# A guard inside the sum of squares, and a bank for each block of the last product

## The chip, the cores and the metric

The kernel runs on one core of a Trainium2 chip. The metric is the device time of one execution in microseconds (us). The engines are named as in the profile: PE (TensorE matmuls), PEld (its weight loads), DVE (VectorE), ACT (ScalarE), POOL (GpSimd), SP (SyncE, which issues most transfers).

## The reference

One step of a one-layer decoder over 2112 tokens (64 sample tokens and 2048 prompt tokens) of width 1024: a mixer of two kinds of linear recurrences, then a squared-ReLU MLP, then a final norm. What the change touches is the end of the layer and that norm:

```python
def rmsnorm(x, w):
    xf = x.astype(jnp.float32)
    r = xf * lax.rsqrt(jnp.mean(xf * xf, axis=-1, keepdims=True) + NORM_EPS)
    return (r * w.astype(jnp.float32)).astype(x.dtype)
...
        xp = xp + mp
        hp = rmsnorm(xp, norm_ffn_w[l])
        xp = xp + jnp.square(jax.nn.relu(hp @ w_up[l])) @ w_down[l]
...
    y_prompt = rmsnorm(xp, final_norm_w)
```

The guard of the last norm is `NORM_EPS` (1e-6).

## The kernel before, in words

**Layout.** Tokens are columns, features are partitions (8 blocks of 128). The tokens come in three groups of T = 512, 832 and 768. Each group runs through mixer, output projection (`out_proj`), MLP (`ffn`) and final norm. Weights and activations are held as two float32r parts (hi, lo), and each product is three matmuls (hi·hi, hi·lo, lo·hi). Work tiles are slabs of [128, 832] float32 out of a pool of 42. PSUM has a pool `pj` of two tiles of two banks each and a pool `mm` of four tiles of one bank.

**The scaled residual.** The norm ahead of the MLP is not applied to its input. Let q be mean(x²) + eps of the residual x. The squared ReLU of the unnormed input, multiplied by w_down, is q times too large, so the residual is multiplied by q instead (`scale_residual_first`, `scale_residual`), and everything after it carries the factor q. In the last norm this factor drops out of x/√mean(x²) but not out of the guard. The kernel before keeps g.r = 1/q (four reciprocals of a quarter each for every group, `inverse`), and `last_factor` multiplies the sum of squares by g.r² (L1662), takes Ln and Exp with the guard eps (L368, L369) and multiplies the result by g.r (L1664).

**The down product.** For groups 1 and 2 (`down`) the MLP's products are done by Strassen-like octets: for each of four octets seven products, each of two tiles v = 0, 1 with two blocks i = 0, 1 of 128 rows and T/2 = 384 columns (group 2). A tile [128, 2, 512] of `pj` holds the two blocks in two banks. DVE adds a finished tile to the accumulated rows (`put`, L1558). The last octet's order ends with S3·T3, A22·T4 and A12·B21; the last one completes the first half (h = 0) of feature blocks 0 to 3, A22·T4 that of blocks 4 to 7, S3·T3 the second half (h = 1). In the very last product of the kernel (`end`) each block is added for itself (L1588) so that its square (L1682) can start.

**Order.** The program is written with an agenda: `later(ticks, fn)` runs fn after so many ticks, and two matmuls make one tick, so one product of `down` is 24 ticks. The framework then orders the instructions of each engine by their place in the program and their readiness, and sets all waits.

**The final norm.** For groups 0 and 1 `finish_first` and `finish` run beside the next group's mixer. For group 2 `finish(g, (1,), 1)` treats h = 1 beside the last two products, with its adds of squares on POOL (L1625), the split of the sum into two parts (L1407, L1408), four matmuls with ones (L1416), the factor, and per block a multiplication by weight and factor (L1642) with a transfer for each pair of blocks (L1644). `finish_last` treats h = 0: squares and weights of each block on ACT (L1682, L1683), adds on POOL (L1685), the split (L498, L499), sums by matmul (float32r for six blocks, L1695, float32 for the last two, L1696), the factor, eight multiplications on DVE and POOL (L1705) and eight transfers (L1706).

Of the kernel before, what the change touches and what calls it, by code (L numbers as in the profile page):

```python
# [207 lines left out]
class Kernel:  # L208
# [972 lines left out]
    def scale_residual_first(self, g):  # L1181
# [19 lines left out]

        def inverse(i):
            if not i:
                g.r = self.get()
            c = slice(i * T // 4, (i + 1) * T // 4)
            nc.vector.reciprocal(g.r[:, c], x["q"][:, c])

# [4 lines left out]
        self.later(112, mean)  # L1212
        for i in range(4):
            self.later(194 + 20 * i, inverse, i)

# [36 lines left out]
    def finish_first(self, g):  # L1252

        nc, T = self.nc, g.T
        x = {"sum": None}

# [107 lines left out]
    def scale_residual(self, g):  # L1364
# [24 lines left out]

        def inverse(i):  # L1390
            if not i:
                g.r = self.get()
            c = slice(i * T // 4, (i + 1) * T // 4)
            nc.vector.reciprocal(g.r[:, c], x["q"][:, c])

# [6 lines left out]
        for i in range(4):  # L1402
            self.later(520 + 10 * i, inverse, i)

# [143 lines left out]
    def down(self, g, plan, nxt):  # L1548
# [14 lines left out]
        for o in range(NO):  # L1563
            last = o == NO - 1
            for A, B, first, into in LAST_OCTET if last else OCTET:
                self.plan_steps(plan, k, 0, 24)
                end = nxt is None and k == 7 * NO - 1
                if last and k % 7 == 3 and nxt is not None:
                    self.norm_in(nxt)
                if nxt is None and k == 7 * NO - 2:  # L1570
                    self.finish(g, (1,), 1)
                if end:
                    self.finish_last(g, 0)
                if first:
                    banks = [self.pj.tile([P, 2, 512], F32, tag="pj", name="pd")[:, :, :T2] for _ in range(2)]
                for v in range(2):
                    w = self.next_weight()
                    for i in range(2):
                        for e in range(2):
                            for f in range(2):  # L1580
                                c = (2 * e + f) * 256 + i * P
                                for q, (a, b) in enumerate(((0, 0), (0, 1), (1, 0))):
                                    self.matmul(banks[v][:, i], w[a][:, c:c + P], self.pair(g, g.d[o][e][B][b])[:, f],
                                                start=first and e == f == q == 0, stop=e == f == 1 and q == 2,
                                                skip_group_check=not first)
                        if end:
                            r = self.last_block(g, 2 * v + i, 0)
                            nc.vector.tensor_tensor(out=r, in0=banks[v][:, i], in1=r, op=ALU.add)  # L1588
                    if not end:
                        for q in into:  # L1590
                            put(v, "copy" if k == 0 else q, banks[v])
# [22 lines left out]

    def finish(self, g, hs=(0, 1), per=None):

# [4 lines left out]
        def square(np_, h):  # L1621
            t = self.get()
            nc.scalar.activation(t[:, :T], g.R[np_ % 2][np_ // 2, h][:, :T], AF.Square)
            if h in x:
                (nc.gpsimd if per else nc.vector).tensor_tensor(out=x[h][:, :T], in0=x[h][:, :T], in1=t[:, :T], op=ALU.add)  # L1625
            else:
                x[h] = t

        def split(h):
            x["parts", h] = self.pair_parts(g, x[h])  # L1630
            x["t", h] = self.get()
            nc.scalar.activation(x["t", h][:, :T2], g.r[:, h * T2:(h + 1) * T2], AF.Square)

        def factor(h):
            t = x["t", h][:, :T2]
            self.last_factor(g, self.pair_sums(g, x["parts", h]), t, t, h * T2, (h + 1) * T2, 0 if per else 4)

# [7 lines left out]

        pace, wait, gap, each = (3, 8, 6, 3) if per else (4, 8, 10, 5)
        t1 = 1 + pace * len(todo)
        for k, (np_, h) in enumerate(todo):
            self.later(1 + pace * k, square, np_, h)
            self.later(t1 + wait + gap + each * k, out, np_, h)  # L1650
        for h in hs:
            self.later(t1 + 2 * h, split, h)
            self.later(t1 + wait + 2 * h, factor, h)

# [4 lines left out]

    def last_factor(self, g, ps, r2, t, c0, c1, lag=0):  # L1660

        self.nc.vector.tensor_tensor(out=r2, in0=ps, in1=r2, op=ALU.mult)  # L1662
        self.rsqrt(t, r2, r2, self.eps, D)
        times = lambda: self.nc.vector.tensor_tensor(out=t, in0=t, in1=g.r[:, c0:c1], op=ALU.mult)  # L1664
        self.later(lag, times) if lag else times()

# [3 lines left out]

    def finish_last(self, g, h):

        nc, w = self.nc, g.T // 2
        order = (4, 5, 6, 7, 0, 1, 2, 3)
        when = [1, 2, 3, 4] + [7, 13, 19, 25]
        n_sum = KB - 2
        x = {}

        def square(k):
            n = order[k]  # L1680
            acc, t = self.last_block(g, n, h), self.get()
            nc.scalar.activation(t[:, :w], acc, AF.Square)  # L1682
            nc.scalar.activation(acc, acc, AF.Copy, scale=self.vec[:, V_FIN + n:V_FIN + n + 1])  # L1683
            if 0 < k < n_sum:
                nc.gpsimd.tensor_tensor(out=x[0][:, :w], in0=x[0][:, :w], in1=t[:, :w], op=ALU.add)  # L1685
            else:
                x[k] = t
            if k == n_sum - 1:
                x["parts"] = self.parts(x[0][:, :w], w)

        def sums(k):
            if k == n_sum:
                x["ps"] = self.mm(w)
                for j, part in enumerate(x["parts"]):
                    nc.tensor.matmul(x["ps"], self.ones_r, part, start=j == 0, stop=False)  # L1695
            nc.tensor.matmul(x["ps"], self.ones, x[k][:, :w], start=False, stop=k == KB - 1)  # L1696

        def outs():
            r2, t = self.get(), self.get()
            nc.scalar.activation(r2[:, :w], g.r[:, h * w:(h + 1) * w], AF.Square)  # L1700
            self.last_factor(g, x["ps"], r2[:, :w], t[:, :w], h * w, (h + 1) * w)
            for n in range(KB):
                acc = self.last_block(g, n, h)
                eng = nc.gpsimd if n % 3 == 2 else nc.vector
                eng.tensor_tensor(out=acc, in0=acc, in1=t[:, :w], op=ALU.mult)  # L1705
                nc.sync.dma_start(self.outputs(g, h)[:, n], acc)  # L1706

        for k in range(KB):
            self.later(when[k], square, k)
            if k >= n_sum:  # L1710
                self.later(when[k] + (11 if k < KB - 1 else 5), sums, k)
        self.later(when[-1] + 10, outs)


# [58 lines left out]
```

## Time and profile before

| | |
|---|---|
| median of 3 runs | 2588.03 us (2586.77 to 2589.51) |
| profiled execution | 2586.12 us |
| its span, first to last instruction | 2584.3 us |
| mean granted TensorE clock | 0.997 |
| busy: PE, PEld, DVE, ACT, POOL | 98%, 93%, 65%, 45%, 30% |

How to read it: the profile is one execution with a record of every instruction. Busy times are sums over the whole span. A line such as L1642 is a line of the kernel before; `out<-in` are the program's names of the tiles. The chain that ended last is followed back from the last instruction, at each step to what released it. In a timeline a bracket gives the idle time of the engine just before an instruction and what ended it.

### The profile page before, as it was taken

How to read it: one execution, taken by the hardware profiler on the slowest of the kernel's cores; microseconds unless marked ns; L12 is line 12 of the kernel's file. 1: busy time of each engine (PE TensorE's matmuls, PEld its weight loads, DVE VectorE, ACT ScalarE, POOL GpSimd, SP SyncE). 2: the span in 40 equal slices, each digit the busy share in tenths (PEclk: the TensorE clock that was granted, in tenths of full speed). 3: DMA queues.
4: the chain of work that ended last, by engine and by line, in shares of the span. 5: the costliest groups of instructions: out<-in, count | busy, mean ns of one | idle time of the engine just before them, and what ended most of it. 6: DMA issues, size and time to landing. Idle time of an engine off the chain costs nothing. (4 is left out here: it accounts for less than half of the span.)

```text
span 2584.3 us, 37190 instructions
## 1 busy us (share of the span) xinstructions
PE 2538.6 (98%) x14689; PEld 2404.1 (93%) x14689; DVE 1688.4 (65%) x2122; ACT 1166.5 (45%) x1575; POOL 772.3 (30%) x480
## 2 busy tenths in 40 slices
PE   8999999999999999999999999999999999999997
PEld 6888788888999999999999999999999999999997
DVE  6666776556666576646655977875556465559886
ACT  6666533234434343345434444454444354345443
POOL 5655251111234143201222322242244012223222
PEclk9999999999999999999999999999999999999999
DMA  7556755554264655613456555442222325565452
GB/s 256 207 201 210 279 202 195 192 195 161 98 220 158 225 202 170 230 72 136 167 169 228 206 174 177 149 160 82 99 108 100 120 90 179 183 218 194 171 180 82
DMA packets 146237, 442.33 MB, mean 171 GB/s; under 512 B 14736, under 2 KB 36240, under 8 KB 146064
## 3 DMA queue, kind: packets, MB, share of 16 engines
q1 hardware_dynamic: 145920, 439.94, 48.8%
q8 instruction: 116, 1.90, 0.3%
q14 instruction: 57, 0.47, 0.1%
q10 hardware_dynamic: 144, 0.02, 0.0%
HBM read 331.11 MB, written 108.79 MB: 170 GB/s over the span
## 5 line engine op out<-in xcount | busy, mean ns | idle before, releaser
L352 PE MATMUL pj<-slab,hi 128*128 128x416 f32 (+2 forms) x2844 | 742.4, 364 | 6.3 <-ACT hi L277 5.9
L277 ACT CAST hi<-raw 128x1024 fp32r<-128x1024 f32 x330 | 346.7, 1051 | 677.9 <-PE pu L1145 191.6
L292 POOL TENSOR_TENSOR lo<-raw,hi 128x1024 fp32r<-128x1024 f32 x119 | 314.7, 2645 | 933.9 <-ACT hi L277 866.4
L352 PEld LDWEIGHTS pj<-slab,hi 128*128 128x128 f32 x2844 | 514.3, 189 | 39.1 <-ACT hi L277 5.9
L1145 PE MATMUL pd<-slab,hi 128*128 128x416 f32 (+1 forms) x1792 | 469.5, 342 | 5.1 <-DVE slab L1588 3.1
L352 PE MATMUL pj<-slab,lo 128*128 128x416 f32 (+2 forms) x1422 | 435.6, 364 | 0.1
L1145 PE MATMUL pu<-slab,hi 128*128 128x416 f32 (+1 forms) x1600 | 408.1, 342 | 0.0
L292 DVE TENSOR_TENSOR lo<-raw,hi 128x1024 fp32r<-128x1024 f32 x211 | 269.5, 1277 | 188.7 <-ACT hi L277 188.2
L1145 PEld LDWEIGHTS pd<-slab,hi 128*128 128x128 f32 x1792 | 329.4, 188 | 8.7 <-DVE slab L1588 3.7
L1145 PE MATMUL pd<-slab,lo 128*128 128x416 f32 (+1 forms) x896 | 307.9, 344 | 0.0
L1145 PEld LDWEIGHTS pu<-slab,hi 128*128 128x128 f32 x1600 | 294.0, 188 | 1.5
L352 PEld LDWEIGHTS pj<-slab,lo 128*128 128x128 f32 x1422 | 259.9, 189 | 17.2 <-issue 1.9
L1145 PE MATMUL pu<-slab,lo 128*128 128x416 f32 (+1 forms) x800 | 264.2, 343 | 0.0
L352 PE MATMUL mm<-slab,hi 128*128 128x512 f32 x740 | 229.5, 390 | 0.0
L727 PE MATMUL pjv<-hi,slab 128*128 128x256 f32 x1088 | 211.9, 286 | 1.0 <-ACT slab L737 1.0
L1344 DVE TENSOR_TENSOR slab<-slab 128x832 fp32r<-128x832 f32 (+1 forms) x144 | 162.9, 1148 | 37.4 <-ACT slab L1340 18.1
L727 PEld LDWEIGHTS pjv<-hi,slab 128*128 128x128 f32 x1088 | 174.2, 190 | 3.0 <-ACT slab L737 1.4
L1340 ACT CAST slab<-slab 128x832 fp32r<-128x832 f32 (+1 forms) x144 | 122.0, 860 | 116.7 <-DVE slab L1351 83.1
L1145 PEld LDWEIGHTS pd<-slab,lo 128*128 128x128 f32 x896 | 168.1, 188 | 0.5
L352 PEld LDWEIGHTS mm<-slab,hi 128*128 128x128 f32 x740 | 138.5, 188 | 29.2 <-ACT slab L1175 0.4
L727 PE MATMUL pjv<-lo,slab 128*128 128x256 f32 x544 | 153.8, 283 | 0.0
L1145 PEld LDWEIGHTS pu<-slab,lo 128*128 128x128 f32 x800 | 149.7, 188 | 0.5
(205 smaller groups left out, 3708.3 us busy)
## 6 DMA issues: line engine op xcount, KB each, us to landing
raw<-w SPq DMA_DIRECT2D x270, 512.0 KB, 4.1
u<-ld SPq DMA_DIRECT2D x32, 416.0 KB, 4.2
slab<-u SPq DMA_DIRECT2D x32, 416.0 KB, 5.7
u<-ld SPq DMA_DIRECT2D x32, 384.0 KB, 4.6
slab<-u SPq DMA_DIRECT2D x32, 384.0 KB, 4.9
ld<-x SPq DMA_DIRECT2D x16, 416.0 KB, 4.8
ld<-x SPq DMA_DIRECT2D x16, 384.0 KB, 4.0
raw<-su1S SPq DMA_DIRECT2D x8, 512.0 KB, 3.9
```

The costliest lines, as they stand in the source:

```text
L277: self.nc.scalar.copy(hi, raw)
L292: eng.tensor_tensor(out=lo, in0=self.second.pop(j), in1=hi.bitcast(F32), op=ALU.subtract)
L352: self.nc.tensor.matmul(pj[:, i, :T2], w, a[:, c0:c1], start=j == 0 and q == 0, stop=j == n - 1 and q == 2)
L727: nc.tensor.matmul(pj[:, i * 256:(i + 1) * 256], a[:, s:s + C], ww, start=kb == 0 and q == 0, stop=kb == KB - 1 and q == 2)
L1145: self.nc.tensor.matmul(*a, **k)
L1340: self.nc.scalar.copy(hi[:, :g.T], B[name][:, :g.T])
L1344: self.nc.vector.tensor_tensor(out=lo[:, :g.T], in0=B[name][:, :g.T], in1=hi.bitcast(F32)[:, :g.T], op=ALU.subtract)
```

## The change

- The guard: `last_guard` makes one slab g.e = q² · EPS · D / P with one ACT operation for each group, in place of the four reciprocals. Summed over the 128 partitions with the squares it adds D · EPS · q² to the sum, which is the guard that the factor q asks for. So `last_factor` is Ln straight from the bank and Exp, with no DVE operation. In `finish_first` g.e is the start of the sum; in `finish` and `last_rows` it is added to the first square.
- The half h = 1 of the last group starts one product earlier (at S3·T3), with its adds on DVE and ticks of its own.
- `last_rows` (new) squares blocks 4 to 7 of h = 0 a pair at a time during the last product and weighs them.
- `last_product` (new) takes the last product out of the loop: two of its blocks go to `mm` tiles, two to `pj` tiles, each block to a tile of its own.
- `finish_last` squares blocks 0 and 1 together, adds on DVE, splits, and brings in blocks 2 and 3 by float32 matmuls; the outputs are four multiplications of a pair of blocks, all on DVE, with four transfers.

The diff, without the unchanged surroundings:

```diff
@@ scale_residual_first (and the same in scale_residual, there at tick 520 for 520 + 10 i)
-        def inverse(i):
-            if not i:
-                g.r = self.get()
-            c = slice(i * T // 4, (i + 1) * T // 4)
-            nc.vector.reciprocal(g.r[:, c], x["q"][:, c])
+        def guard():
+            self.last_guard(g, x["q"])
...
-        for i in range(4):
-            self.later(194 + 20 * i, inverse, i)
+        self.later(194, guard)
@@ finish_first
-        x = {"sum": None}
+        x = {"sum": g.e}
...
         def factor():
-            r2, x["t"] = self.get(), self.get()
-            nc.scalar.activation(r2[:, :T], g.r[:, :T], AF.Square)
+            x["t"] = self.get()
             for (c0, c1), ps in zip(g.pieces, self.both_sums(g, x["parts"])):
-                self.last_factor(g, ps, r2[:, c0:c1], x["t"][:, c0:c1], c0, c1, 4)
+                self.last_factor(ps, x["t"][:, c0:c1])
@@ down
+                if nxt is None and k == 7 * NO - 3:
+                    self.finish(g, (1,), True)
                 if nxt is None and k == 7 * NO - 2:
-                    self.finish(g, (1,), 1)
+                    self.last_rows(g)
                 if end:
-                    self.finish_last(g, 0)
+                    self.last_product(g, B)
+                    break
...
-                        if end:
-                            r = self.last_block(g, 2 * v + i, 0)
-                            nc.vector.tensor_tensor(out=r, in0=banks[v][:, i], in1=r, op=ALU.add)
+    def last_product(self, g, B):
+        nc, T2 = self.nc, g.T // 2
+        w = [self.next_weight(), self.next_weight()]
+        banks = [self.mm(T2) for _ in range(2)]
+        banks += [self.pj.tile([P, 2, 512], F32, tag="pj", name="pd")[:, 0, :T2] for _ in range(2)]
+        self.finish_last(g)
+        for v in range(2):
+            for i in range(2):
+                ps = banks[2 * v + i]
+                for e in range(2):
+                    for f in range(2):
+                        c = (2 * e + f) * 256 + i * P
+                        for q, (a, b) in enumerate(((0, 0), (0, 1), (1, 0))):
+                            self.matmul(ps, w[v][a][:, c:c + P], self.pair(g, g.d[NO - 1][e][B][b])[:, f],
+                                        start=e == f == q == 0, stop=e == f == 1 and q == 2)
+                r = self.last_block(g, 2 * v + i, 0)
+                nc.vector.tensor_tensor(out=r, in0=ps, in1=r, op=ALU.add)
@@ finish
-                (nc.gpsimd if per else nc.vector).tensor_tensor(out=x[h][:, :T], in0=x[h][:, :T], in1=t[:, :T], op=ALU.add)
+                nc.vector.tensor_tensor(out=x[h][:, :T], in0=x[h][:, :T], in1=t[:, :T], op=ALU.add)
             else:
                 x[h] = t
+                nc.vector.tensor_tensor(out=t[:, :T2], in0=t[:, :T2], in1=g.e[:, h * T2:(h + 1) * T2], op=ALU.add)
...
+        if last:
+            for k, (np_, h) in enumerate(todo):
+                self.later((2, 8, 14, 26)[k], square, np_, h)
+                self.later((41, 50, 59, 73)[k], out, np_, h)
+                if k == 3:
+                    self.later(28, split, h)
+                    self.later(35, factor, h)
+            return
@@ last_factor
-        self.nc.vector.tensor_tensor(out=r2, in0=ps, in1=r2, op=ALU.mult)
-        self.rsqrt(t, r2, r2, self.eps, D)
-        times = lambda: self.nc.vector.tensor_tensor(out=t, in0=t, in1=g.r[:, c0:c1], op=ALU.mult)
-        self.later(lag, times) if lag else times()
+    def last_guard(self, g, q):
+        g.e = self.get()
+        self.nc.scalar.activation(g.e[:, :g.T], q[:, :g.T], AF.Square, scale=(EPS * D / P) ** 0.5)
+    def last_factor(self, ps, t):
+        self.nc.scalar.activation(t, ps, AF.Ln, scale=1.0 / D)
+        self.nc.scalar.activation(t, t, AF.Exp, scale=-0.5)
+    def last_rows(self, g):
+        def square(v):
+            t = self.get()
+            nc.scalar.activation(t[:, :T], g.R[v][1, 0][:, :T], AF.Square)
+            if v:
+                nc.vector.tensor_tensor(out=g.sq[:, :T], in0=g.sq[:, :T], in1=t[:, :T], op=ALU.add)
+            else:
+                g.sq = t
+                nc.vector.tensor_tensor(out=t[:, :T2], in0=t[:, :T2], in1=g.e[:, :T2], op=ALU.add)
+        def weigh(n):
+            r = self.last_block(g, n, 0)
+            nc.scalar.activation(r, r, AF.Copy, scale=self.vec[:, V_FIN + n:V_FIN + n + 1])
+        for v in range(2):
+            self.later(13 + 13 * v, square, v)
+            for i in range(2):
+                self.later(17 + 13 * v + 2 * i, weigh, 4 + 2 * v + i)
@@ finish_last
+        def squares():
+            t = x["sum"] = self.get()
+            nc.scalar.activation(b2(t), self.pair(g, g.R[0][0, 0]), AF.Square)
+            nc.vector.tensor_tensor(out=b2(t), in0=b2(t), in1=self.pair(g, g.sq), op=ALU.add)
+        def split():
+            x["parts"] = [b2(s) for s in (self.getr(), self.getr())]
+            nc.scalar.copy(x["parts"][0], b2(x["sum"]))
+            nc.vector.tensor_tensor(out=x["parts"][1], in0=b2(x["sum"]), in1=x["parts"][0].bitcast(F32), op=ALU.subtract)
+        def square(n):
+            x[n] = self.get()
+            nc.scalar.activation(x[n][:, :w], block(n), AF.Square)
+        def sums():
+            for part in x["parts"]:
+                for i in range(2):
+                    nc.tensor.matmul(x["ps"], self.ones_r, part[:, i], start=False, stop=False)
+        def add(n):
+            if n == 2:
+                x["ps"] = self.mm(w)
+            nc.tensor.matmul(x["ps"], self.ones, x[n][:, :w], start=n == 2, stop=n == 3)
+        def outs():
+            t = self.get()
+            self.last_factor(x["ps"], t[:, :w])
+            for np_ in range(4):
+                r = self.pair(g, g.R[np_ % 2][np_ // 2, 0])
+                nc.vector.tensor_tensor(out=r, in0=r, in1=t[:, :w].unsqueeze(1).to_broadcast([P, 2, w]), op=ALU.mult)
+                nc.sync.dma_start(self.outputs(g, 0)[:, 2 * np_:2 * np_ + 2], r)
+        for d, fn, *a in ((13, squares), (14, weigh, 0), (15, weigh, 1), (17, split), (19, square, 2), (23, add, 2),
+                          (25, square, 3), (26, weigh, 2), (27, weigh, 3), (28, sums), (29, add, 3), (30, outs)):
+            self.later(d, fn, *a)
```

More of the change, by code (lines that the diff above doesn't have):

```diff
@@ L1388, in scale, with guard @@
                                     in1=x["q"][:, h * T2:(h + 1) * T2].unsqueeze(1).to_broadcast([P, 2, T2]))
[L1390 to L1394, printed above, removed]
+        def guard():
+            self.last_guard(g, x["q"])
         for k, (h, v, m) in enumerate((h, v, m) for h in range(2) for v in range(2) for m in range(2)):
@@ L1401, in scale_residual @@
             self.later(310 + 10 * h, mean, h)
-        for i in range(4):
-            self.later(520 + 10 * i, inverse, i)
+        self.later(520, guard)
     def pair_parts(self, g, s):
@@ L1585, in down @@
                                                 skip_group_check=not first)
-                        if end:
-                            r = self.last_block(g, 2 * v + i, 0)
[L1588 to L1591, printed above, removed]
+                    for q in into:
+                        put(v, "copy" if k == 0 else q, banks[v])
                 if last and A == "S2":
@@ L1669, in last_block, with finish_last, weigh @@
         return self.pair(g, g.R[np_ % 2][np_ // 2, h])[:, i]
-    def finish_last(self, g, h):
+    def finish_last(self, g):
         nc, w = self.nc, g.T // 2
-        order = (4, 5, 6, 7, 0, 1, 2, 3)
-        when = [1, 2, 3, 4] + [7, 13, 19, 25]
-        n_sum = KB - 2
         x = {}
[L1679 to L1692, printed above, removed]
+        b2 = lambda t: t[:, :2 * w].rearrange("p (i t) -> p i t", i=2)
+        block = lambda n: self.last_block(g, n, 0)
+        def weigh(n):
+            nc.scalar.activation(block(n), block(n), AF.Copy, scale=self.vec[:, V_FIN + n:V_FIN + n + 1])
+        def squares():
[15 more added lines that the diff above has]
+            if n == 2:
@@ L1701, in outs @@
[L1701 to L1711, printed above, removed]
```

25 lines of the change are left out of this document (8 added, 17 removed).

## The prediction

> **What bounds the kernel now.** I read the page first, then the chain that ended last, then the timeline of each engine over the last 30 us, and at the end the stretches (busy time by window) in which the other edits lie.
>
> ```profile
> span 2584.3 us, 37190 instructions
> PE 2538.6 (98%) x14689; PEld 2404.1 (93%) x14689; DVE 1688.4 (65%) x2122; ACT 1166.5 (45%) x1575; POOL 772.3 (30%) x480
> ```
>
> PE is busy for 2538.6 of 2584.3 us, so an edit to another engine pays only where PE waits, or after PE's last product. The profiled execution took 2586.12 us, 1.82 us more than its span; the median of the runs is 2588.03, so I work out a difference against this execution and put it on the median. A difference of 0.2%, 5.2 us, is about what a measurement of this kernel can tell from no change.
>
> The chain, with start, length, and what ran (first and last pieces of the end):
>
> ```profile
> 2399.35 158.01 PE pd L1145 x910
> ...
> 2560.48 3.70 DVE slab L1642 x4
> ...
> 2564.65 2.87 DVE slab L1642 x4
> ...
> 2568.49 0.53 ACT slab L1682
> ...
> 2569.16 1.02 POOL slab L1685
> ...
> 2570.20 0.52 ACT slab L498
> ...
> 2570.74 0.57 DVE slab L499
> ...
> 2571.80 1.50 PE mm L1696 x4
> ...
> 2573.40 0.57 DVE slab L1662
> ...
> 2573.99 0.62 ACT slab L368
> ...
> 2574.64 0.53 ACT slab L369
> ...
> 2575.20 0.57 DVE slab L1664
> ```
>
> For 158 us the chain is PE's products alone; from 2560.48 it is not PE but DVE: the output multiplications of half 1 (L1642, 6.57 us) stand in DVE's queue ahead of the adds that empty the last product's banks. PE shows the other end of that:
>
> ```profile
> 2557.19 0.86 PE L1416 MATMUL mm<-slab,ones_r 128*128 128x384 f32 x4
> ...
> 2558.25 0.52 PE L1145 MATMUL pd<-slab,hi 128*128 128x384 f32 x2
> ...
> 2562.25 0.34 PE L1145 MATMUL pd<-slab,lo 128*128 128x384 f32 x1
> 2564.71 0.61 PE L1145 MATMUL pd<-slab,hi 128*128 128x384 f32 x2 [2.12 <-DVE slab L1588]
> ...
> 2568.05 0.61 PE L1145 MATMUL pd<-slab,hi 128*128 128x384 f32 x2 [0.96 <-DVE slab L1588]
> ...
> 2570.09 0.34 PE L1145 MATMUL pd<-slab,lo 128*128 128x384 f32 x1
> ```
>
> The last product is 48 matmuls in four blocks of 12. The first 24 run without a break from 2558.25 to about 2562.42, 0.1737 us each. The third and the fourth block wait for L1588 (2.12 and 0.96 us). That fits only if PE runs block 0 of each tile first and then block 1 of each: the two blocks of a tile share one accumulator tile of two banks, and the second may not write until L1588 has read the first. The last matmul ends at 2570.43.
>
> **Part by part. The banks.** Each block now has a tile of its own, so nothing that DVE does can hold PE between blocks. 48 matmuls at 0.1737 are 8.34 us; the last ends near 2558.25 + 8.34 + 0.17 = 2566.8, not 2570.43: **3.65 us** are gone (the two waits, and the slower matmul pairs after them, 0.61 for 0.52). What is late next is DVE, which must now do in 8 us what it did in 12.
>
> **Half 1's norm**, moved 24 ticks forward with all its squares, sums, factor, eight multiplications and four output transfers; its adds go from POOL to DVE.
>
> ```profile
> 2553.33 0.84 ACT L1407 CAST slab<-slab 128x768 fp32r<-128x768 f32 x1 [2.07 <-POOL slab L1625]
> 2554.20 0.96 DVE L1408 TENSOR_TENSOR slab<-slab 128x768 fp32r<-128x768 f32 x1 [2.60 <-ACT slab L1407]
> 1697.25 4.01 DVE L1642 SCALAR_TENSOR_TENSOR slab<-slab,vec 128x416 f32<-128x416 f32 x7
> ```
>
> The parts of the sum are ready at 2555.16 now, behind a POOL add; with the add on DVE (0.95 us, as wide as L1408) I put them at about 2554.3. Their four matmuls (0.7 us on PE) are written at the eleventh tick of the product before the last, which begins near 2558.25 - 8.34 - 0.7 = 2549.2, so PE comes to them at 2553.0. Queued behind them on PE is the rest of that product. If the order keeps that place, PE waits up to 1.3 us; if they are ordered when ready, nothing. The trace of before has squares that run as soon as their rows are complete, so the order follows readiness, and I take 0.35. The factor is then two ACT operations in place of DVE, two ACT, DVE, and the eight multiplications start some 4 us earlier, near 2556.5. Undisturbed they take 0.57 each (seven in 4.01, a little wider), 4.6 us in all against 6.57, because POOL's adds no longer run beside them. They are done before 2564 even with the adds of the last product between them, and half 1's transfers are far from the end. On SP nothing else is in the way there.
>
> **The last half's chain.** Rows for what comes after the last matmul:
>
> ```profile
> 2575.79 4.49 DVE L1705 TENSOR_TENSOR slab<-slab 128x384 f32<-128x384 f32 x6
> 2575.83 2.63 POOL L1705 TENSOR_TENSOR slab<-slab 128x384 f32<-128x384 f32 x2 [5.66 <-DVE slab L1664]
> 2577.22 3.99 SPq L1706 DMA_DIRECT2D y<-slab  x8
> L1705 DVE TENSOR_TENSOR slab<-slab x6: 544/550/1347, 2575.8 to 2579.7; 128x384 f32<-128x384 f32 x6
> DMA to landing us min/median/max: 1.9/2.0/2.1
> DMA to landing us min/median/max: 2.4/2.6/7.7
> 2522.36 2.69 DVE L1561 TENSOR_TENSOR slab<-slab 128x768 f32<-128x768 f32 x3
> ```
>
> (The first landing row is that of L1706, 192 KB each; the second that of L1644, 384 KB each, the size of the new transfers.) Now, from the last matmul at 2570.43: block add, square, two fp32 products, L1662, two ACT, L1664, and at 2575.79 the outputs. New:
> - DVE in the last 8 us has, beside the multiplications, four block adds (0.55), two adds of squares and the split (0.9 each) and the guard's add (0.55). The queue as I place it: the first two blocks' matmuls end at 2562.6, their adds, with multiplications between, at 2563.7; the square of both on ACT (0.84, as wide as L1407) at 2564.5; its add on DVE at 2565.45, block 2's add at 2566.0; ACT's split of the sum at 2566.4 and block 2's square behind it at 2566.9; the split's subtraction on DVE from 2566.4 to 2567.3. So the last add ends at 2567.85, 0.5 us later than its matmul alone would allow.
> - Its square (0.53) to 2568.4. Meanwhile PE has the fp32 product of block 2 (half of the 1.50) and the four fp32r sums (0.7) behind it, so block 3's product starts near 2568.6 and ends at 2569.4.
> - Ln straight from the bank and Exp, 0.62 + 0.53 with gaps: 2570.6. L1662 and L1664 (0.57 each) are gone: the guard is in the sum.
> - Four multiplications of 768 columns on DVE, 0.9 apart (three in 2.69): 2570.6 to 2574.2. The old stage took 4.49, because two of DVE's six took 1347 ns where the others took 544: those beside POOL's two (2575.83, 2.63 us). The new stage leaves POOL out, 3.6 us. The Trainium skill (GPSIMD Engine Reference, 1. Specifications) says that the SBUF interfaces are shared with VectorE and that instructions with two SBUF inputs contend; by that rule the estimate is the 3.6; if the 1347 ns had another cause that stays, two slow ones would add 1.6 and make 5.2. The trace agrees with the rule, 544 beside nothing and 1347 beside POOL.
> - The last transfer: now the last multiplication ends at 2575.79 + 4.49 = 2580.28, but SP's eight issues end at 2577.22 + 3.99 = 2581.21 and the span 3.1 us later. Four issues keep up with DVE: the last is issued by 2574.7, 6.5 us earlier. It is twice as large and lands 0.6 later (2.6 for 2.0). [...]
>
> So the tail gives -6.5 + 0.6 = **-5.9**, plus 0.35 for half 1's sums: **-5.6 us**.
>
> **Everything in the middle.** The guard's square replaces reciprocals:
>
> ```profile
> L1206 DVE RECIPROCAL slab<-slab x4: 894/920/953, 363.2 to 367.4; 128x128 f32<-128x128 f32 x4
> L1394 DVE RECIPROCAL slab<-slab x8: 1294/1370/1446, 1339.2 to 2265.9; 128x208 f32<-128x208 f32 x4, 128x192 f32<-128x192 f32 x4
> 40.00:290.00 250.00, 234.88 (x1412) 199.93 (x1411) 160.85 (x305) 156.32 (x260) 137.46 (x105) 0.98 0.61 213
> 360.00:370.00 10.00, 10.00 (x46) 8.29 (x45) 9.12 (x12) 2.11 (x2) 2.52 (x2) 1.00 0.38 134
> 665.00:705.00 40.00, 40.00 (x236) 39.69 (x236) 21.63 (x26) 16.21 (x18) 9.62 (x5) 1.00 0.37 132
> 705.00:1070.00 365.00, 358.24 (x2415) 345.31 (x2414) 250.39 (x386) 152.56 (x228) 130.36 (x107) 1.00 0.58 199
> 1335.00:1350.00 15.00, 15.00 (x82) 14.86 (x81) 11.94 (x11) 6.27 (x7) 2.40 (x1) 1.00 0.49 166
> 1665.00:1705.00 40.00, 39.98 (x227) 39.39 (x226) 31.02 (x38) 23.08 (x27) 6.93 (x3) 1.00 0.45 154
> 1705.00:2060.00 355.00, 355.00 (x2490) 350.26 (x2489) 198.41 (x340) 157.84 (x240) 111.22 (x81) 1.00 0.29 107
> ```
>
> Columns: window, its length, busy PE, PEld, DVE, ACT, POOL, clock. DVE loses 4 x 0.92 + 8 x 1.37 = 14.6 us; ACT gains three squares (a row as wide, L1407, took 0.84). PE is the cover: it is busy for 10.00 of 10.00 us and 15.00 of 15.00 where reciprocals of groups 0 and 1 stand. The factors of groups 0 and 1 (665 to 705, 1665 to 1705) lose two DVE products and a square for each piece and gain one add for each; PE is busy for 40.00 and 39.98 of 40. All of it at 0. Less work cannot uncover PE by itself; what can is another order of the engines' queues, and the mixers right behind show what that is worth: the mixer of group 0 lets PE wait for 15.1 of 250 us, that of group 1 for 6.8 of 365, that of group 2 for none in 355. Bounds for groups 1 and 2 together: from -6.8 (as group 2's) to +8.3 for one (15.1 - 6.8) and up to 15 for the other. I take 0: no edit puts a new wait there, and the rows say nothing of which way an order would fall.
>
> **The rivals.**
> - *PE's queue is held at the end.* The fp32 product of block 2 is written two matmuls ahead of the end, at about 2566.4, and needs a square that by my queue is done at 2566.9; if split and square come later on DVE and ACT, PE waits with two matmuls, and then the last add, behind it. For it: DVE has little idle time there. Price: the product's 0.8 plus a wait of about 0.5, with half 1's sums waiting the full 1.3: -5.9 + 1.3 + 1.3 = -3.3, and -4.6 if only the product is held.
> - *The waits only change place.* The adds of the last blocks stand behind multiplications and splits on DVE as before, and the end comes from DVE: the 3.65 of the banks is lost, the chain's 2.3 stays, about -2.
> - *The mixer falls better*: group 1's 6.8 us shrink, -8 to -12.
> - *Slower: the mixer falls worse.* With other times of DVE and ACT at the start of groups 1 and 2, a mixer gets the order in which PE waits for DVE or ACT in its small products. Price: up to 15.1, as in group 0. It decides from 5.6 us of new waits; one mixer at group 0's 15.1 would give +2.7 to +9.5 in all. Against it: the edits take work away there, and PE is ahead of nothing new.
>
> **How the numbers follow.** Forecast (-5.6, its own range -4.8 to -6.6): 0.52. Held queue (-3.3): 0.19. Waits change place (-2): 0.07. Better mixer (-8 to -12): 0.10. Worse mixer: 0.12, half of it beyond +5.2. Faster by over 0.2%: 0.42 of the forecast's 0.52 and the better mixer, 0.52. Slower by over 0.2%: 0.06. Between: 0.42. Time: 2588.03 - 5.6 = 2582.4. Range: from -9.5 (half of the better mixer) to -2 (the held queue and half of the changed places): 2578.5 to 2586.0; a little under 0.2 is left out, most of it above.
>
> **What would show it.** Right: no wait of PE for the last product's adds; the last matmul near 2566.8 on the old clock; Ln directly behind PE's last fp32 product; four output multiplications of about 0.95 us and nothing on POOL; mixers with 6.8 and 0 us of waits. Wrong: PE waiting for ACT's square or for half 1's split; the last add late behind DVE's other work; PE busy less than 358 of 365 us in group 1's mixer or less than 355 in group 2's.

## The result, and the profile after

| | before | after |
|---|---|---|
| median | 2587.84 us (16 runs, 2585.62 to 2592.84) | 2581.82 us (16 runs, 2579.53 to 2584.67) |
| ratio | | 0.9976, 95% interval 0.9968 to 0.9983 |
| profiled execution, span | 2586.12, 2584.3 us | 2582.45, 2580.7 us |

The change saves 6.0 us (4.4 to 8.3 by the interval); 5.6 were forecast (2582.4 us). The two profiled executions differ by 3.7 us only: before's is one of its faster ones, after's one of its slower ones. So I compare the stage in which the change acts. I call **tail** the time from the add of the first tile of S3·T3 on DVE to the end of the span. Ahead of it PE is busy for 145.00 of 145 us, before from 2400 and after from 2402.6, so what the change does at the end lies in the tail. The row that starts the tail, from DVE's timeline, before:

```profile
2545.26 0.96 DVE L1558 TENSOR_TENSOR slab<-pd,slab 128x768 f32<-128x768 f32 x1 [1.98 <-PE pd L1145]
```

and DVE's timeline after, from that row to the end of the span at 2580.67 (line numbers are those of the kernel after; L1549 was L1558, L1651 was L1642, L1605 was L1588, L1753 was L1705):

```profile
2547.86 0.96 DVE L1549 TENSOR_TENSOR slab<-pd,slab 128x768 f32<-128x768 f32 x1 [0.24 <-PE pd L1145]
...
2559.45 2.20 DVE L1651 SCALAR_TENSOR_TENSOR slab<-slab,vec 128x384 f32<-128x384 f32 x4
...
2562.44 1.14 DVE L1651 SCALAR_TENSOR_TENSOR slab<-slab,vec 128x384 f32<-128x384 f32 x2
...
2564.83 0.61 DVE L1651 SCALAR_TENSOR_TENSOR slab<-slab,vec 128x384 f32<-128x384 f32 x1
...
2568.89 0.96 DVE L1732 TENSOR_TENSOR slab<-slab 128x768 fp32r<-128x768 f32 x1 [0.46 <-ACT slab L1731]
2569.76 0.55 DVE L1605 TENSOR_TENSOR slab<-pd,slab 128x384 f32<-128x384 f32 x1
2572.95 3.56 DVE L1753 TENSOR_TENSOR slab<-slab 128x768 f32<-128x768 f32 x4 [2.64 <-ACT slab L1685]
```

The tail is 2584.30 - 2545.26 = 39.04 us before and 2580.67 - 2547.86 = 32.81 after: **-6.23**. The medians differ by 6.02, which leaves 0.2 us, well within the interval, for everything ahead of the tail. Half 1's multiplications (L1651) now lie early and in small groups between the adds, four in 2.20 us where four took 3.70 before. The last add (L1605) follows its product at once.

The chain that ended last, after:

```profile
2557.68 3.66 PE pd L1145 x21
2561.34 4.16 PE mm L1145 x24
2565.50 4.17 PE pd L1145 x24
2569.66 0.65 PE mm L1746 x2
2570.31 0.69 PE mm L1741 x4
2571.01 0.85 PE mm L1746 x2
2571.87 0.50 ACT slab L1684
...
2572.40 0.53 ACT slab L1685
...
2572.95 0.96 DVE slab L1753
2573.91 0.87 DVEq L1800
```

It is PE's alone up to 2571.87: the last product's 48 matmuls run in 8.33 us without a break, first two banks of `mm`, then two of `pj`, then block 2's fp32 product (L1746), the four sums (L1741) and block 3's. Ln (L1684) reads the bank right behind it, and the outputs follow Exp. Before, the same chain ran through DVE's multiplications and POOL's adds.

The middle, in the stretches of the mixers of groups 1 and 2, after (columns as in the prediction: window, length, busy PE, PEld, DVE, ACT, POOL, clock):

```profile
705.00:1070.00 365.00, 358.13 (x2399) 344.65 (x2399) 243.63 (x375) 149.82 (x226) 133.81 (x107) 1.00 0.58 198
1705.00:2060.00 355.00, 355.00 (x2489) 350.26 (x2488) 197.02 (x339) 157.70 (x240) 110.94 (x81) 1.00 0.30 106
```

PE is busy for 358.13 and 355.00 us, 358.24 and 355.00 before: no new wait of PE, and none gone, though DVE does 6.8 us less in the first stretch. In the profiled execution the tail starts 2.60 us later than before's; the last section shows where most of that comes from.

### The profile page after: what moved, and what is told of

Same layout as the page of the kernel before. It is cut to its first block, busy times and chain, and to the rows that moved or that the text cites. A ratio compares the mean times of both kernels' runs of the same rounds, so it can differ in the third digit from the quotient of the medians.

```text
span 2580.7 us, 37147 instructions
## 1 busy us (share of the span) xinstructions
PE 2540.8 (98%) x14691; PEld 2407.0 (93%) x14691; DVE 1669.4 (65%) x2108; ACT 1165.7 (45%) x1570; POOL 760.4 (29%) x470
```

## The experiments

Each kernel's tail is cut at its first output multiplication: "to outputs" is what PE, DVE, POOL and ACT do up to there, "outputs" the rest. All are worked out from the rows shown above for before and after, in each kernel's own trace, so each tail is that of one execution; the outputs show how well such a figure repeats where the code is the same (8.51 to 8.53 in seven kernels, 7.71 to 7.74 in five). Each ratio is against runs of before on the same chip. The kernels were timed on several chips, so ratios rather than medians are compared from row to row; two kernels have one time only.

| kernel | to outputs | outputs | tail | median | ratio (95%) |
|---|---|---|---|---|---|
| before | 30.53 | 8.51 | 39.04 | 2587.84 | |
| banks_only | 31.32 | 8.53 | 39.85 | 2588.52 | 1.0002 (0.9993 to 1.0012) |
| banks_warm | 29.88 | 8.53 | 38.41 | 2588.21 once | |
| guard_only | 28.78 | 8.51 | 37.29 | 2587.13 | 0.9994 (0.9985 to 1.0003) |
| early_half | 28.41 | 8.52 | 36.92 | 2586.70 | 0.9993 (0.9983 to 1.0002) |
| banks_early | 26.77 | 8.52 | 35.29 | 2583.90 | 0.9984 (0.9975 to 0.9993) |
| old_final | 25.57 | 8.53 | 34.10 | 2582.68 | 0.9980 (0.9971 to 0.9990) |
| after | 25.09 | 7.72 | 32.81 | 2581.82 | 0.9976 (0.9968 to 0.9983) |
| shared_banks | 26.96 | 7.71 | 34.67 | 2584.28 | 0.9985 (0.9975 to 0.9994) |
| late_half | 27.56 | 7.71 | 35.27 | 2585.40 | 0.9987 (0.9978 to 0.9997) |
| no_guard | 27.07 | 7.74 | 34.81 | 2583.76 | 0.9982 (0.9972 to 0.9991) |
| small_last | 25.10 | 7.63 | 32.73 | 2582.73 | 0.9981 (0.9971 to 0.9991) |
| small_first | 25.08 | 7.54 | 32.62 | 2582.78 | 0.9982 (0.9973 to 0.9992) |
| two_queues | 25.07 | 7.73 | 32.80 | 2583.67 once | |

**The banks alone** (banks_only: before, with a bank for each block):

```diff
+                if end:
+                    own = [self.mm(T2) for _ in range(2)] + [b[:, 0] for b in banks]
...
+                        ps = own[2 * v + i] if end else banks[v][:, i]
...
-                            nc.vector.tensor_tensor(out=r, in0=banks[v][:, i], in1=r, op=ALU.add)
+                            nc.vector.tensor_tensor(out=r, in0=ps, in1=r, op=ALU.add)
```

> The kernel before with one part of the change: each block of the last product has a bank of its own (two mm tiles, two pj tiles); guard, half 1 and the final sums as before. Tail = from the add of S3·T3's first tile to the end of the span, 39.0 us before, 32.8 after the whole change. My theory: PE waits for no add in the last product, its last matmul comes 3.65 us earlier, but DVE's queue (8 multiplications of half 1, slowed by POOL's adds) and POOL's adds then end last, so the tail keeps 2 to 3.7 of it: 35.3 to 37.0 us. Rival, the waits only change place: under 1 us of gain, 38 us or more.

The tail grew to 39.85: the rival. PE's wait at the end (who waited <- for whom: us in all, times, longest), and its windows there (window, length, busy PE, PEld, DVE, ACT, POOL, granted clock, which is 1.00 at full speed):

```profile
PE mm L1698 <- ACT slab L498: 3.5, 1, 3.5
...
2571.40:2574.90 3.50, 0.04 (x1) 0.00 (x0) 2.23 (x5) 1.62 (x4) 0.99 (x1) 1.00 0.58 219
2575.40:2578.90 3.50, 3.22 (x6) 1.44 (x5) 0.14 (x2) 1.80 (x4) 0.00 (x0) 0.54 0.00 0
```

The waits between the blocks are gone, and one of 3.5 us stands behind the product, for the split of the sum (L498). DVE shows why:

```profile
2565.18 3.71 DVE L1645 SCALAR_TENSOR_TENSOR slab<-slab,vec 128x384 f32<-128x384 f32 x4
...
2569.28 2.96 DVE L1645 SCALAR_TENSOR_TENSOR slab<-slab,vec 128x384 f32<-128x384 f32 x4
...
2572.62 1.01 DVE L1591 TENSOR_TENSOR slab<-pd,slab 128x384 f32<-128x384 f32 x2
```

Half 1's multiplications hold the adds (L1591) until 2573.6 whether the banks wait for them or not. That the tail grew has a second cause: PE, idle for 3.5 us, came back at a granted clock of 0.54, and the four fp32 products took 2.57 us on the chain where before's took 1.50. To see what that alone costs, 18 matmuls whose result is never read were put into the idle time (banks_warm):

```diff
+                        if end and v == i == 1:
+                            fill = self.mm(T2)
+                            for j in range(18):
+                                nc.tensor.matmul(fill, self.ones_r, self.pair(g, g.d[o][0][B][0])[:, j % 2], start=j == 0, stop=j == 17)
```

> The kernel with the banks alone, and 18 matmuls with ones into a spare bank (never read) behind the last product. There PE stood idle for 3.55 us waiting for ACT, and the four float32 matmuls after it took 2.57 us where the kernel before has 1.50. My theory: the granted clock fell to half in that idle time, and with PE kept busy the four take 1.5 again: tail about 38.8 (39.85 without the filler). Rival, they are slow for another reason, a wait inside: 39.8.

In its PE timeline the filler fills the gap, and the products are fast again:

```profile
2569.34 3.28 PE L1592 MATMUL mm<-slab,ones_r 128*128 128x384 f32 x18
2573.08 1.04 PE L1702 MATMUL mm<-slab,ones_r 128*128 128x384 f32 x2 [0.45 <-ACT slab L498]
2573.95 1.45 PE L1703 MATMUL mm<-slab,ones 128*128 128x384 f32 x4
```

The tail is 1.44 shorter than with the banks alone (38.41). So at a full clock the banks by themselves are worth -0.6, and in this execution the clock takes that back and 0.8 more. How much of a stretch at half clock falls on these products differs between executions (last section); by its ten runs banks_only can't be told from before.

**The guard alone** (guard_only: before, with `last_guard`, the short `last_factor` and the guard's add; the last half otherwise as before):

```diff
...
-            self.last_factor(g, x["ps"], r2[:, :w], t[:, :w], h * w, (h + 1) * w)
+            self.last_factor(x["ps"], t[:, :w])
...
```

> The kernel before with the guard in the sum of squares in all three groups (one ACT square instead of four reciprocals, factor = Ln and Exp from the bank), everything else as before. My theory: nothing in the middle (mixer of group 1 with 6 to 8 us of PE waits, of group 2 with none); in the tail the two DVE products of 0.57 leave the last chain, -1.2, and half 1's factor comes 1.1 us earlier, which takes as much from PE's wait of 2.12 for the first block add: tail 36.5 to 37.0. Rival, only the last chain counts: 37.8. Rival, the mixers fall otherwise: group 1's waits change by more than 3 us.

-1.75, between the two. Two products on DVE with their gaps are gone from both factors. In half 1's factor that brings its multiplications forward too, and the waits between the blocks shrink from 3.1 to 2.7 us:

```profile
PE pd L1145 <- DVE slab L1573: 2.7, 2, 1.4
```

**Half 1 early, alone** (early_half: before, with the earlier start, its ticks and its adds on DVE):

```diff
-                if nxt is None and k == 7 * NO - 2:
+                if nxt is None and k == 7 * NO - 3:
...
-                (nc.gpsimd if per else nc.vector).tensor_tensor(out=x[h][:, :T], in0=x[h][:, :T], in1=t[:, :T], op=ALU.add)
+                nc.vector.tensor_tensor(out=x[h][:, :T], in0=x[h][:, :T], in1=t[:, :T], op=ALU.add)
...
```

> The kernel before with one part of the change: half 1's norm started one product earlier, with the change's ticks and its adds on DVE; banks, guard and the final half as before. Tail from the add of S3·T3's first tile to the end of the span: 39.0 before, 39.9 with the banks alone, 32.8 with the whole change. My theory: DVE's queue of half 1's multiplications is what held PE, so with them done earlier PE's waits for the block adds fall from 3.1 to about 1 us even with shared tiles, and nothing else changes: tail 36.5 to 37. Rival, POOL's adds of half 0 end last in any case, as with the banks alone: 38.5 or more.

-2.12, as expected, with one wait of 1.7 us left where about 1 was expected. The edit does two things, the earlier start and the adds moved from POOL to DVE; no run has one of them alone on the kernel before. The row of the wait and the row of DVE that explains it (POOL's adds of half 0 run beside these four):

```profile
PE pd L1145 <- DVE slab L1588: 1.7, 1, 1.7
...
2564.45 4.03 DVE L1642 SCALAR_TENSOR_TENSOR slab<-slab,vec 128x384 f32<-128x384 f32 x4
```

**Both together** (banks_early: the edits of banks_only and early_half, guard and last half as before). Alone the banks cost 0.8; if the parts stand in series, they must pay here:

> The kernel before with a bank for each block and with half 1 one product earlier (its adds on DVE); guard and last half as before. Tail measured from the DVE add of the first tile of S3·T3 to the end of the span: before 39.04, banks alone 39.85, early half alone 36.92 us. Theory (the parts stand in series: the banks pay once DVE's queue is free of half 1's multiplications): the one wait that the early half alone leaves, 1.7 us, goes, and with it the slower pairs behind it, some 0.2; POOL's adds and the two products after the last matmul stay. Tail 34.8 to 35.4 us, that is 1.5 to 2.1 below the early half alone, although the banks alone cost 0.8. Rival (the parts simply add, and the banks alone are worth +0.8 for another reason): about 37.7 us. Between: PE must wait for the split of the sum, with POOL's adds late, 36 us or more.

35.29: 1.63 below the early half alone. All that PE still waits for at the end is one wait of 0.2 us:

```profile
PE mm L1706 <- DVE slab L499: 0.2, 1, 0.2
```

So the same edit is worth +0.8 or -1.6 (-0.6 alone with PE kept at full clock), and what decides is whether DVE is free when the blocks are done and whether PE is left idle long enough to lose its clock.

**The last half as before** (old_final: after, with before's `finish_last`, its POOL adds, and eight outputs on DVE and POOL with eight transfers):

```diff
-                if nxt is None and k == 7 * NO - 2:
-                    self.last_rows(g)
...
-                nc.tensor.matmul(x["ps"], self.ones_r, part[:, i], start=False, stop=False)
+                nc.gpsimd.tensor_tensor(out=x[0][:, :w], in0=x[0][:, :w], in1=t[:, :w], op=ALU.add)
...
-            for np_ in range(4):
+            for n in range(KB):
+                eng = nc.gpsimd if n % 3 == 2 else nc.vector
...
```

> The changed kernel with the final half done as in the kernel before (squares by block, adds on POOL, two float32 products behind the last matmul, eight multiplications on DVE and POOL, eight transfers); banks, guard and the early half 1 as changed. My theory: POOL's first output multiplication (1.36 us) holds the first transfer in SP's queue 0.45 longer than a pair on DVE, both float32 products lie behind the last matmul (0.3), and the rest of POOL's adds is hidden: tail 33.3 to 33.8. Rival, POOL's adds slow half 1's multiplications again and end last: 34.8 or more.

+1.29, between the two: 0.48 up to the outputs and 0.81 in them. With that, four kernels each add one part to the one ahead: early half -2.12, banks -1.63, guard -1.19, last half -1.29. That they add up to -6.23 follows from the way they are built; what they show is the size of each part in this order, and another order has other sizes.

**Each part taken out of the whole.** The banks shared again (shared_banks):

```diff
-        banks = [self.mm(T2) for _ in range(2)]
-        banks += [self.pj.tile([P, 2, 512], F32, tag="pj", name="pd")[:, 0, :T2] for _ in range(2)]
+        two = [self.pj.tile([P, 2, 512], F32, tag="pj", name="pd")[:, :, :T2] for _ in range(2)]
+        banks = [two[v][:, i] for v in range(2) for i in range(2)]
```

> The changed kernel with the banks undone: the last product writes two pj tiles of two banks as before. My theory: half 1's multiplications now start earlier and run without POOL, so DVE's queue is short and PE waits for block adds 0.5 to 1.5 us in all: tail 33.3 to 34.3 (32.8 with own banks). Rival, the banks alone carry the 3.65: tail about 36.5.

+1.86, somewhat beyond the 33.3 to 34.3 expected, with the waits that were expected. PE's waits at the end, and DVE's second and third add:

```profile
PE pd L1145 <- DVE slab L1605: 0.9, 1, 0.9
PE mm L1746 <- ACT slab L1736: 0.4, 1, 0.4
...
2566.99 1.02 DVE L1605 TENSOR_TENSOR slab<-pd,slab 128x384 f32<-128x384 f32 x2 [1.45 <-PE pd L1145]
```

DVE being free, the wait between the blocks is 0.9 and not 3.1. The rest lies behind it: PE takes block 0 of both tiles first while DVE's adds go by block number, so DVE waits 1.45 us for PE before its second add, and the squares (L1736) come later. Half 1 one product later again, with before's ticks (late_half):

```diff
-                if nxt is None and k == 7 * NO - 3:
+                if nxt is None and k == 7 * NO - 2:
...
-                self.later((2, 8, 14, 26)[k], square, np_, h)
-                self.later((41, 50, 59, 73)[k], out, np_, h)
+                self.later(1 + 3 * k, square, np_, h)
+                self.later(27 + 3 * k, out, np_, h)
...
```

> The changed kernel with half 1's norm started one product later, at the ticks of the kernel before (adds still on DVE). My theory: its 8 multiplications (0.55 each, 4.4 us) fall into the last product beside the adds and splits of half 0, and the last add or the split comes 1 to 2 us later: tail 33.8 to 34.8. Rival, DVE has room for them anyway: tail within 0.3 of 32.8.

+2.46, more than either expected. Its waits, and PE's last product in its windows:

```profile
PE mm L1746 <- ACT slab L1736: 2.0, 1, 2.0
...
2570.30:2571.60 1.30, 1.25 (x2) 0.11 (x1) 0.00 (x0) 0.01 (x1) 0.00 (x0) 0.50 0.00 0
```

A wait there was expected. What I missed is that the clock halves behind it (0.50): block 3's fp32 product takes some 1.3 us there, 0.85 in after. Without the guard (no_guard: reciprocals, products and the long factor as before):

```diff
...
-            self.last_factor(x["ps"], t[:, :w])
+            r2, t = self.get(), self.get()
+            nc.scalar.activation(r2[:, :w], g.r[:, :w], AF.Square)
+            self.last_factor(g, x["ps"], r2[:, :w], t[:, :w], 0, w)
```

> The changed kernel with the guard undone: reciprocals, the two products of the factor on DVE and its square are back in all groups. My theory: the two DVE products with their gaps (1.2) and a Ln that reads SBUF (0.62 for 0.49) return to the last chain, half 1's later factor is hidden: tail 34.1 (32.8 with the guard), PE waits of the mixers as in the changed kernel. Rival, the reciprocals and half 1's factor count too: 35 or more, or mixers with other waits.

+2.0, between the two. The end of its chain:

```profile
2572.22 0.57 DVE slab L1694
...
2572.81 0.62 ACT slab L368
...
2573.46 0.53 ACT slab L369
...
2574.01 0.57 DVE slab L1696
```

From the last product to the outputs 2572.12 to 2574.60, 2.48 us, against 1.10 in after (2571.85 to 2572.95): 1.38 of the 2.0. The other 0.6 lies ahead of it: half 1's factor is longer as well, DVE's queue later, and PE waits 0.3 for block 2's square.

**The outputs.** Before's bytes and after's over time in the stretches 2576 to 2585 and 2573 to 2582, in 40 slices of 0.225 us each (GB/s), each behind a row of SP's queue. Before, the wait ahead of its first issue (the issues run from 2577.22 to 2581.21):

```profile
SPq L1706 <- POOL slab L1705: 9.2, 1, 9.2
...
GB/s 0 0 0 0 0 0 0 0 0 253 382 369 341 389 369 348 267 369 369 362 362 369 382 341 376 389 335 389 232 0 0 0 0 0 0 0 0 36 0 0
```

After, its four issues:

```profile
2573.94 2.98 SPq L1754 DMA_DIRECT2D y<-slab  x4
...
GB/s 0 0 0 0 0 0 0 0 287 389 348 314 417 348 362 362 369 369 376 328 375 382 348 369 389 369 369 123 0 0 0 0 0 0 0 0 0 0 0 0
```

Eight transfers or four, the 1.57 MB take the same 20 slices, 4.5 us, most of them at 330 to 390 GB/s. From the first issue to the last landing it is 5.70 us in both (2577.22 to 2582.92, 2573.94 to 2579.64). After's issues end at 2576.92 and its bytes run on to 2579.3: the transfers set the pace, not the issues. Three kernels test what is left. The last pair split (small_last):

```diff
-            for np_ in range(4):
+            for np_ in range(3):
...
+            for n in (6, 7):
+                nc.vector.tensor_tensor(out=block(n), in0=block(n), in1=t[:, :w], op=ALU.mult)
+                nc.sync.dma_start(self.outputs(g, 0)[:, n], block(n))
```

> The changed kernel with its last output pair as two multiplications and two transfers of 192 KB. My theory: the last transfer lands 0.6 earlier for 0.1 more on DVE: tail 32.3. Rival, SP's issue of the extra transfer takes the place of it: 32.8.

32.73, the rival: a smaller last transfer saves nothing that counts, since it only stands in the same stream. The first pair split instead (small_first, the same edit at n = 0, 1):

> The changed kernel with its FIRST output pair as two multiplications and two transfers of 192 KB. In all nine kernels so far 5.7 us pass from the issue of the first of the last outputs to the landing of the last, whether they are eight, five or four transfers. Theory, the transfers bound that stage: the first is issued after one multiplication of 384 columns, 0.4 us earlier, and the end comes 0.4 us earlier: tail 32.4 (32.8 changed, 32.7 with the last pair split). Rival, DVE and the size of the last transfer set the end, as in the prediction: tail 32.9, 0.1 later for the extra multiplication.

32.62, half of what the theory has. SP's queue:

```profile
2579.66 0.82 SPq L1753 DMA_DIRECT2D y<-slab  x2
2581.03 2.07 SPq L1757 DMA_DIRECT2D y<-slab  x3
```

The first issue comes 0.59 us after the first multiplication starts (2579.07), 0.99 in after; but from there to the end it takes 6.95 us, 6.73 in after, and 0.2 is left. Outputs in turns on the queues of SP and ACT (two_queues):

```diff
-                nc.sync.dma_start(self.outputs(g, 0)[:, 2 * np_:2 * np_ + 2], r)
+                (nc.scalar if np_ % 2 else nc.sync).dma_start(self.outputs(g, 0)[:, 2 * np_:2 * np_ + 2], r)
```

> The changed kernel with its four last output transfers issued in turn by SP and ACT. Theory, the bytes take their time on the DMA engines (393 KB in 1.05 us, landing after landing): nothing changes, tail within 0.1 of 32.8, 5.7 us from the first issue to the last landing. Rival, one issuing queue hands them out one after the other: the landings draw together and the stage falls to about 5 us, tail near 32.1.

No change (32.80). None of the three is told from after by its ratio, and none beats it.

## Why the prediction was right

Times of after are put on before's clock by taking off 2.60.

- **The banks, -3.65 and +0.35 for half 1's sums.** The last matmul ends at 2569.66 - 2.60 = 2567.06, where 2566.8 + 0.35 was forecast, and 2570.43 before. PE has no wait between blocks or for half 1's sums as such; but from the add of S3·T3's second tile to the last product it takes 9.16 us (2552.02 to 2561.18) where it took 8.83 (2549.42 to 2558.25), and these 0.33 are the 0.35, which was a choice between nothing and 1.3, so that its fit is luck. The term is right as a step of the whole and wrong as a price of the edit: alone the banks are worth +0.8. What the prediction books for the banks is what banks and early half bring together, -2.12 - 1.63 = -3.75; it named DVE's queue of half 1 as what held PE, and gave the early start no price of its own.
- **DVE's queue.** The last add was put 0.5 late, at 2567.85, and with the 0.35 at 2568.2. It ends at 2570.31 - 2.60 = 2567.71: this was the mis-sized term, by 0.5, as the subtraction of the split (L1732) was done 0.4 earlier than I placed it and the add followed it without a gap. With it the outputs start at 2570.35 where 2570.95 was forecast. This makes up nearly all of the difference between the -5.55 of the sum and the measured -6.23.
- **Ln and Exp straight from the bank.** Near the forecast: 1.10 us from the last product to the outputs, 1.2 forecast. The whole guard is worth 1.2 on top of the early half and the banks, 2.0 taken out of the whole.
- **Four multiplications, 3.6 us.** 3.56. Half 1's multiplications, as wide as before, take 2.20 for four with POOL idle and 3.70 where two of the four run beside its adds (1.36 each, the others 0.61). The Trainium skill (GPSIMD Engine Reference, 1. Specifications) says that GpSimd shares its SBUF interfaces with VectorE and that the two contend where a VectorE instruction has two SBUF inputs. These rows agree with it once more.
- **SP's eight issues and the last transfer's size.** The sum was right (outputs 8.51 to 7.72; 7.8 forecast), its reason not. Issues do not set the end, since the stream takes 4.5 us either way. What pays is that the first issue comes 0.44 earlier behind the first multiplication (1.43 to 0.99), and some 0.35 behind the last landing (1.38 us to the end of the span before, 1.03 after). Before, SP waits for POOL's first multiplication, which ends at 2577.19, though DVE's first is done at 2576.35. The longer stretch behind the last landing is seen in before, banks_early and old_final, all with eight transfers and POOL's multiplications; with five transfers (small_last, small_first) it is no longer than with four, and no run separates its cause. A larger last transfer cost nothing: split, it saves 0.08. So the 0.6 that the forecast sets against it fits by luck: from the end of SP's last issue to the end of the span it is 3.09 before and 3.76 after, because the last transfer stands behind the three ahead of it.
- **The middle, 0.** As forecast; neither mixer rival came (PE waits 6.9 and 0 us in the two mixers). That after's tail starts 2.60 later in its profile goes for more than half on a clock that its execution lost (last section).
- **Held queue.** In after PE never waits at the end, but it was close: without the guard it waits 0.3 us for a square, with shared banks 0.4, with half 1 late 2.0.
- **Waits change place.** This rival did not come for the whole change, and it is just what the banks alone do.

## What to carry to other kernels

Where several queues end within a few microseconds of each other, an edit has no price of its own: the same banks were +0.8, -1.6 or -1.9 with three different neighbours, in one profile each. Before giving a waiting engine room, look at what the engine that it waited for still has to do; if that stands unchanged, the wait moves to the next product. And for a train of output transfers at the end, first look at when its first byte leaves, then at the size or number of the rest.

## What the runs showed of the hardware

A short idle time of PE can cost twice, once for itself and once at half the clock behind it. In after the gap ahead of L788 (a small product in group 1's mixer), with two windows of 3.41 us, the one that holds the gap and the one behind it (columns as above):

```profile
1050.34 0.33 PE L788 MATMUL mm<-con,slab 128*128 128x128 f32 x1 [1.88 <-ACT slab L792]
...
1048.09:1051.50 3.41, 1.53 (x10) 1.19 (x10) 3.41 (x4) 2.16 (x4) 0.80 (x1) 1.00 0.89 365
1051.50:1054.91 3.41, 3.41 (x15) 3.31 (x14) 1.15 (x3) 0.00 (x0) 0.00 (x0) 0.50 0.69 229
```

The same in the kernel with half 1 late:

```profile
1049.14 0.33 PE L788 MATMUL mm<-con,slab 128*128 128x128 f32 x1 [1.89 <-ACT slab L792]
...
1047.57:1050.98 3.41, 1.83 (x13) 1.83 (x14) 3.41 (x5) 2.15 (x4) 0.12 (x1) 1.00 0.89 339
1050.98:1054.40 3.42, 3.42 (x22) 3.40 (x21) 1.98 (x4) 0.00 (x0) 0.54 (x1) 1.00 0.48 162
```

The gap is as long in both, 1.9 us; in one PE goes on at half its clock for 3.4 us, in the other at full clock. The traces show what goes with it. In each of the 14 the changes of the clock lie a whole number of 3.413 us apart, to a few ns, as on a fixed grid. In nine of them the whole gap, 1.88 us, falls into one window of this grid, as in after, and the next window ran at half clock; in the other five the gap is shorter or a grid line splits it (late_half: 0.31 and 1.58 us), one window holds at most 1.67 us of it, and the clock stayed. In before the gap is of the shorter kind:

```profile
1049.31 0.33 PE L788 MATMUL mm<-con,slab 128*128 128x128 f32 x1 [1.43 <-ACT slab L792]
```

After comes to this product 1.03 us later than before and loses up to 1.7 us more at half clock behind it (half of 3.41): at 1090 us the same instructions of PE come 2.59 us later, and the tail starts 2.60 later. The Trainium skill (TensorE: Matmul & The Clock Gate, Part 1: The HAM clock gate) gives such windows as 3413 ns long and free-running, with half a clock after at least one idle window. Length, grid and half clock agree with the traces here, but PE need not be idle for a whole window: 1.88 us of 3.41 were enough.

A share of the scatter of some 5 us between executions of one kernel may come from this: after's sixteen spans go from 2577.7 us at a mean clock of 0.997 to 2582.9 at 0.995. That is a fit of the two, not a test.
